# Decay sums with a stationary triangle, and a higher priority for the small inverses, in a two-layer hybrid decoder trunk

## The chip, the cores and the metric

The kernel runs as one program on one core of a Trainium2 chip. The metric is the device time of one execution in microseconds (us). Before the change it is 1251.22 us, the median of three runs that lie between 1250.65 and 1251.36 us. One further execution, made under the hardware profiler, took 1249.48 us; all rows of "the profile" come from that one.

## The reference

The reference computes two layers over 256 tokens of width 1024 in float32. Each layer is a half-step SwiGLU, a layer norm, three token mixers on one shared input projection (a gated delta rule, a sliding-window attention with sinks and an attention over a memory), gates and an output projection, a layer norm, a second half-step SwiGLU and a layer norm. The change concerns the gated delta rule with 4 heads. Cut to what matters:

```python
g = -jnp.exp(a_log) * jax.nn.softplus(a + dt_bias)        # log decay, one number per token and head
g = jnp.cumsum(g, axis=-1)                                # within a chunk
decay = jnp.exp(jnp.where(tril, g[..., :, None] - g[..., None, :], NEG_INF))
a = jnp.where(strict, jnp.einsum('bhncd,bhnsd->bhncs', k_beta, k) * decay, 0.0)
sol = lax.linalg.triangular_solve(a + jnp.eye(C), rhs, left_side=True, lower=True, unit_diagonal=True)
qk = jnp.where(tril, jnp.einsum('bhncd,bhnsd->bhncs', q, k) * decay, 0.0)
```

The kernel uses chunks of 128 tokens, so two chunks (c = 0 and 1) per layer. For each head and chunk it needs the 128x128 matrix of decay sums: the sum of g over the tokens that lie after token i and up to token j. That matrix is masked and put through an exponential. The triangular solve is replaced by the explicit inverse of the 128x128 unit triangle, made from its 16x16 blocks by doubling: 16 to 32, 32 to 64, 64 to 128.

## The kernel before

TensorE does nearly everything in products of type fp32r, each float32 matrix split into a high part and a rest: `split` (L124) makes the high part on ScalarE (a cast) and the rest on VectorE (a subtraction), both of type fp32r, and three products stand for one (`mm3`). The weights, 1024 columns of 128 partitions at a time, come through `unit` (L104): a DMA on SyncE's queue into one of four `raw` buffers, then the split into `whi` and `wlo`, which have five buffers each. Its instructions stand 300 places ahead of their place in the program.

The order of the instructions on each engine is worked out at build time by a planner. It simulates the program with its own costs, and whenever an engine is free it takes the ready instruction with the smallest place in the program, where a place can be moved ahead by an offset (`tc.high_priority(offset=...)`). `tc.issue_after` adds single edges of order. On the chip each engine then goes through its list in that order. Within the mixers all products of TensorE are pinned in program order (`pe`, L129, with `pinned[0]` set in `mixers`, L560), so the planner orders only the other engines there. `weave` (L145) runs a large projection as a generator and calls small steps between its parts; that is where the products of the delta rule stand in TensorE's order.

The decay sums. A chain of small operations on VectorE ends in `g` (L718, 128 tokens x 2 chunks x 4 heads). GpSimd then makes, for each chunk, a tile `gm` of 128x4x128 numbers: the strict triangle `mlt` times g of the token, one copy per head (L758). `spread(c)` (L737) runs four float32 products, one per head, with `gm` of that head as the stationary operand and the triangle of ones `tri` as the moving one; the sums land in one `sm` bank of PSUM. VectorE adds the mask (L743), ScalarE takes the exponential (L744). `gm` and the result are the two halves of one tile `TM[c]`, in the buffers `w2` and `w3`. `spread(0)` and `spread(1)` stand at steps 2 and 3 of the last small projection (L976). `products` (L746) then makes the matrices `AK`.

The inverses. `inverses` (L922) makes the 16x16 blocks on GpSimd. `doubling(c)` (L985) has four stages for each chunk; each runs some 32x32 products and then moves the results out of PSUM: a copy on ScalarE (L993), a subtraction and a transposition on VectorE (L999, L1000), copies on ScalarE (L1008), and in the last stage scaled copies on ScalarE (L1017, L1019, L1021) and copies on GpSimd (L1023). `double` (L1028) runs one stage for both chunks. `lower_products` (L1040) and `upper_products` (L1049) do the last step with 64x64 products and copies on ScalarE (L1046, L1047, L1056). They stand between the parts of the second gates' projection and the second branch's projection: stages of `double` at steps 1, 3, 5 and 7 of the gates (L1189), `lower_products` at step 8, `upper_products` inside the branch.

Around the same time run the window attention's probabilities: `w_scores` ends in exponentials and scalings on ScalarE (L860, L863), `w_leave` (L889) transposes on VectorE (L893) and sends the tile to DRAM by GpSimd's DMA queue (L896), `w_back` (L900) reads it back (`pt`, L906), and `w_values` (L908) uses it on TensorE.

Of the kernel before, what the change touches and what calls it, by code (L numbers as in the profile page):

```python
# [10 lines left out]
F32 = mybir.dt.float32  # L11
F32R = mybir.dt.float32r
I32 = mybir.dt.int32
AF = mybir.ActivationFunctionType
ALU = mybir.AluOpType
AX = mybir.AxisListType

P = 128
# [14 lines left out]
MAGIC = 0x5F3759DF  # L33
AHEAD = 300
HOLD = 4


@with_exitstack
def tile_trunk(ctx, tc, x, xT, mem, memT_, wst, lnp, memln, cvw, rows, cst, out):
    nc = tc.nc  # L40
# [3 lines left out]
    pc = ctx.enter_context(tc.tile_pool(name="pc", bufs=1))  # L44
    praw = ctx.enter_context(tc.tile_pool(name="praw", bufs=4))
    pu = ctx.enter_context(tc.tile_pool(name="pu", bufs=1))
# [8 lines left out]
    def nm(s):  # L55
        uid[0] += 1
        return f"{s}_{uid[0]}"
# [4 lines left out]
    def T(pool, shape, tag, dt=F32, bufs=None):  # L62
        pool = pn if pool is pu and tag in NEAR else pool
        kw = {} if bufs is None else {"bufs": bufs}
        return pool.tile(shape, dt, tag=tag, name=nm(tag), **kw)
# [7 lines left out]
    def sm():  # L73
        return T(psS, [P, 512], "sm")

    def load(dst, src):

        tc.keep_in_program_order(nc.sync.dma_start(dst, src))  # L78
# [3 lines left out]
    tri = cs[:, C_TRI:C_TRI + P]  # L82
    mlt = cs[:, C_LT:C_LT + P]
    dtm = cs[:, C_DTM:C_DTM + P]

    def over4(ap):
        return ap.unsqueeze(1).to_broadcast([P, 4, ap.shape[-1]])
# [41 lines left out]
    def pe(ins):  # L129

        return tc.keep_in_program_order(ins) if pinned[0] else ins

    def matmul(*a, **k):
        return pe(nc.tensor.matmul(*a, **k))  # L134
# [330 lines left out]
    def begin(nxt, hT):  # L465
        nxt.first(hT, 0)
        nxt.first(hT, 1)
        nxt.out(0, nxt.bank)
# [91 lines left out]
    def mixers(l, hT, mkT, mv_, post0, post):  # L560
# [122 lines left out]
        sh = [P, 2, 4]  # L683

        def col(tag):
            return T(pu, sh, tag)
# [11 lines left out]
        t = col("spt")  # L698
# [18 lines left out]
        g = col("g")  # L717
# [12 lines left out]
            nc.vector.tensor_scalar(neg1, eg[:, 0, 1, :], -1.0, None, ALU.mult)  # L730
            nc.vector.tensor_tensor(ktok, ktok, ks.unsqueeze(2).to_broadcast([P, 4, P]), op=ALU.mult)

        TM = [T(pu, [P, 2, 4, P], f"w{2 + c}") for c in range(2)]
        AK = [T(pu, [P, 4, 2, P], f"u{12 + c}") for c in range(2)]
        hb = lambda ap: ap.unsqueeze(2).to_broadcast([P, 4, P])

        def spread(c):  # L737

            gm, dt = TM[c][:, 0], TM[c][:, 1]
            ps = sm().rearrange("p (h c) -> p h c", h=4)  # L740
            for h in range(4):
                matmul(ps[:, h, :], gm[:, h, :], tri, start=True, stop=True)
            nc.vector.tensor_tensor(dt, ps, over4(dtm), op=ALU.add)  # L743
            nc.scalar.activation(dt, dt, AF.Exp)  # L744

        def products(c, hh):  # L746
# [6 lines left out]
            for j in range(2):  # L753
                h = 2 * hh + j
                nc.vector.scalar_tensor_tensor(AK[c][:, h], TM[c][:, 1][:, h, :].unsqueeze(1).to_broadcast([P, 2, P]), cS[:, c, h:h + 1], ps[:, j], op0=ALU.mult, op1=ALU.mult)

        for c in range(2):
            nc.gpsimd.tensor_tensor(TM[c][:, 0], over4(mlt), hb(g[:, c, :]), op=ALU.mult)  # L758


        xq = (T(pu, [P, 4, S], "u4", F32R), T(pu, [P, 4, S], "u6", F32R))
# [42 lines left out]
        def x_back():  # L804
            pT = prs[2] = T(p2, [P, 2, 4, 4, 32], "pt")
            for kb in range(2):
                with tc.issue_after(late["pool"]):
                    late["pool"] = nc.gpsimd.dma_start(pT[:, kb].rearrange("p a h x -> p (a h x)"), left_x[0][4 * kb:4 * kb + 4].rearrange("m x a c -> (m x) (a c)")).ins
# [113 lines left out]
        def inverses():  # L922
# [11 lines left out]
            x_back()  # L934
            tm = [t.rearrange("p a h c -> p (a h c)") for t in TM]
            parts = [tm[0][:, 0:512], tm[0][:, 512:1024], tm[1][:, 0:512]]
# [25 lines left out]
        X64, X32, Y32 = (W[:, a:b].rearrange("p (c h i) -> p c h i", c=2, h=4) for a, b in ((0, 512), (512, 768), (768, 1024)))  # L962
        Y = T(pu, [P, 2, 4, P], "w1")
# [21 lines left out]
        def doubling(c):  # L985
            B, M = AK[c][:, :, 0, :], TM[c][:, 1]
            Yc = Y[:, c]
            M32 = M[:, :, 0:32]
            ps = part()
            for h in range(4):  # L990
                for q in qd:
                    matmul(ps[q, h], L32[q, c, h], X32[q, c, h], start=True, stop=True)
            nc.scalar.copy(M32, ps)  # L993
            yield
            ps = part()
            for h in range(4):
                for q in qd:
                    matmul(ps[q, h], M32[q, h], Y32[q, c, h], start=True, stop=True)
            nc.vector.tensor_tensor(Y32[:, c], Y32[:, c], ps, op=ALU.subtract)  # L999
            late["dve"] = nc.vector.transpose(W[:, 512 + c * P:512 + c * P + P], W[:, 768 + c * P:768 + c * P + P]).ins  # L1000
            yield
            pairs = ((qd[0], qd[1]), (qd[2], qd[3]))
            ps = part()
            for h in range(4):
                for e, o in pairs:
                    matmul(ps[o, h], B[e, h, o], X32[e, c, h], start=True, stop=True)
            for e, o in pairs:
                pairs_ = nc.scalar.copy(M[o, :, e], ps[o]).ins  # L1008
            late["pairs"] = pairs_
            yield  # L1010
            ps = part()
            e, o = pairs[0]
            for h in range(4):
                for a, b in pairs:
                    matmul(ps[a, h], M[b, h, a], Y32[b, c, h], start=True, stop=True)
                matmul(ps[o, h], Y32[o, c, h], M[o, h, e], start=True, stop=True)
            nc.scalar.mul(X64[o, c, :, e], ps[o], -1.0)  # L1017
            for q in qd[:2]:
                nc.scalar.copy(X64[q, c, :, q], X32[q, c])  # L1019
            for a, b in (pairs if c == 0 else pairs[::-1]):  # L1020
                nc.scalar.mul(Yc[a, :, b], ps[a], -1.0)  # L1021
            for q in (qd if c == 0 else qd[::-1]):
                late["pool"] = nc.gpsimd.tensor_copy(Yc[q, :, q], Y32[q, c]).ins  # L1023
            yield

        stages = [doubling(c) for c in (1, 0)]

        def double():  # L1028
            for d in stages:
                next(d)  # L1030

        up, dn = slice(0, 64), slice(64, P)

# [5 lines left out]

        def lower_products():  # L1040

            pa, pb = (sm().rearrange("p (h c) -> p h c", h=4) for _ in range(2))
            for h in range(4):
                matmul(pa[dn, h, up], AK[0][up, h, 0, dn], X64[up, 0, h], start=True, stop=True)
                matmul(pb[up, h, dn], AK[1][dn, h, 0, up], Y[dn, 1, h, dn], start=True, stop=True)
            nc.scalar.copy(TM[0][dn, 1, :, up], pa[dn, :, up])  # L1046
            nc.scalar.copy(TM[1][up, 1, :, dn], pb[up, :, dn])  # L1047

        def upper_products():  # L1049

            pa, pb = (sm().rearrange("p (h c) -> p h c", h=4) for _ in range(2))
            for h in range(4):
                matmul(pa[up, h, dn], TM[0][dn, 1, h, up], Y[dn, 0, h, dn], start=True, stop=True)
                matmul(pb[up, h, dn], X64[up, 1, h], TM[1][up, 1, h, dn], start=True, stop=True)
            for c, ps in enumerate((pa, pb)):
                nc.scalar.mul(Y[up, c, :, dn], ps[up, :, dn], -1.0)  # L1056

        def begin_inverse():

# [191 lines left out]
    ps = sm()  # L1251
# [6 lines left out]
    def xres(tb):  # L1258
        load(hres[tb], x[tb * P:(tb + 1) * P, :])

    def small():
        load(rw, rows.rearrange("l r -> (l r)").partition_broadcast(P))
        load(cw, cvw)

    ends = None
    for l in range(NL):
        mT = []
        mid = memory_T(mT, l)
        if l == 0:

            mid[2] = lambda: load(cs, cst)
            more = {4: lambda *a: xres(0), 6: lambda *a: xres(1), 8: lambda *a: small()}
        post = Post(lnp[l, 0, 0], lnp[l, 0, 1], bounce=True)
        f1.rest(hT, 4, [((pu, "u0"), (pu, "u1")), ((pu, "u2"), (pu, "u3"))], post, mid, ends, {} if l else more)
        kv = memory_kv(mT, post)
        if l == 0:
            nc.scalar.activation(nea, rw[:, :, 8:12], AF.Exp)
            nc.vector.tensor_scalar(nea, nea, -1.0, None, ALU.mult)
        post2 = Post(lnp[l, 1, 0], lnp[l, 1, 1])
        mixers(l, post.hT, *kv, post, post2)  # L1280
        f2 = Ffn()
        begin(f2, post2.hT)
        last = l == NL - 1
        post = Post(lnp[l, 2, 0], lnp[l, 2, 1], last)
        f2.rest(post2.hT, 6, [((pu, a), (pu, b)) for a, b in (("u0", "u1"), ("u2", "u3"), ("u4", "u5"), ("u6", "u13"))], post, behind=post2.end)
        ends = post.end
        if not last:
            f1, hT = Ffn(), post.hT
            begin(f1, hT)
# [87 lines left out]
```

## Time and profile before

| What | Value |
|---|---|
| time, median of three runs | 1251.22 us (1250.65 to 1251.36) |
| time of the profiled execution | 1249.48 us |
| its span, first to last instruction | 1247.3 us |
| TensorE matmul busy | 1236.5 us, 99% |
| VectorE, ScalarE, GpSimd busy | 887.6, 655.4, 271.5 us |
| granted TensorE clock | 0.998 |

A row of the timeline gives the start in us from the span's start, the time taken, the engine, the line of the kernel, the operation and its operands, and how many instructions are merged; behind it in brackets the idle time of the engine before it and what ended it. PE is TensorE's matmul, PEld its weight load, DVE VectorE, ACT ScalarE, POOL GpSimd. The ends of matmuls are modelled and they overlap, so the distance between the starts of two neighbouring rows, divided by the count, is what one matmul costs the stream. A float32 product appears as two records, an fp32r product as one. A row of a group gives the count, the busy time, the mean ns of one, and the idle time before; a row of waits gives the time waited in total, the number of waits and the longest one.

### The profile page before, as it was taken

How to read it: one execution, taken by the hardware profiler on the slowest of the kernel's cores; microseconds unless marked ns; L12 is line 12 of the kernel's file. 1: busy time of each engine (PE TensorE's matmuls, PEld its weight loads, DVE VectorE, ACT ScalarE, POOL GpSimd, SP SyncE). 2: the span in 40 equal slices, each digit the busy share in tenths (PEclk: the TensorE clock that was granted, in tenths of full speed). 3: DMA queues.
4: the chain of work that ended last, by engine and by line, in shares of the span. 5: the costliest groups of instructions: out<-in, count | busy, mean ns of one | idle time of the engine just before them, and what ended most of it. 6: DMA issues, size and time to landing. Idle time of an engine off the chain costs nothing.

```text
span 1247.3 us, 18730 instructions
## 1 busy us (share of the span) xinstructions
PE 1236.5 (99%) x6812; PEld 1052.6 (84%) x6812; DVE 887.6 (71%) x1316; ACT 655.4 (53%) x976; POOL 271.5 (22%) x481
## 2 busy tenths in 40 slices
PE   9999999999999999999999999999999999999997
PEld 6888889999878888888888888899988788888886
DVE  6688567887768876665676665769869688666555
ACT  6456545656665544444455554456657644454541
POOL 1232102003751102221012220020046411122100
PEclk9999999999999999999999999999999999999999
DMA  8988866755675848886668886676566566688771
GB/s 296 320 267 279 259 228 202 239 171 179 184 242 169 269 140 257 240 242 220 220 207 241 262 255 216 215 238 207 170 192 214 177 215 213 204 243 240 242 230 74
DMA packets 83275, 276.73 MB, mean 222 GB/s; under 512 B 13776, under 2 KB 15216, under 8 KB 83184
## 3 DMA queue, kind: packets, MB, share of 16 engines
q1 hardware_dynamic: 66320, 232.40, 58.0%
q0 software_dynamic: 16720, 43.02, 12.0%
q8 instruction: 53, 0.87, 0.3%
q14 instruction: 38, 0.31, 0.1%
q10 hardware_dynamic: 144, 0.13, 0.0%
HBM read 253.77 MB, written 21.73 MB: 221 GB/s over the span
## 4 chain that ended last, share of the span: by engine, by line
PE 99%; DMA 0%; DVE 0%; SPq 0%; issue 0%; ACT 0%; DVEq 0%
PE acc L134 88%; PE at L134 4%; PE sm L134 3%; PE sm L137 1%; PE acc L332 1%; PE acc L333 1%; PE acc L335 1%; DMA raw<-in_wst_dram 0%; PE at L137 0%; DVE h L291 0%; DVE h L296 0%; SPq L115 0%; SPq L78 0%; ACT whi L125 0%; DVE bnst L277 0%
## 5 line engine op out<-in xcount | busy, mean ns | idle before, releaser
L125 DVE TENSOR_TENSOR wlo<-raw,whi 128x1024 fp32r<-128x1024 f32 (+2 forms) x405 | 486.4, 1209 | 252.1 <-ACT whi L125 249.7
L125 ACT CAST whi<-raw 128x1024 fp32r<-128x1024 f32 (+2 forms) x405 | 413.4, 1029 | 379.7 <-PE acc L134 293.6
L134 PE MATMUL acc<-whi,hT 128*128 128x512 f32 (+1 forms) x1824 | 559.9, 385 | 0.7 <-ACT whi L125 0.7
L134 PEld LDWEIGHTS acc<-whi,hT 128*128 128x128 f32 x1824 | 339.9, 188 | 70.1 <-ACT whi L125 2.7
L134 PE MATMUL acc<-wlo,hT 128*128 128x512 f32 (+1 forms) x912 | 350.1, 384 | 0.0
L134 PE MATMUL acc<-whi,u 128*128 128x512 f32 x812 | 259.0, 392 | 0.0
L134 PEld LDWEIGHTS acc<-wlo,hT 128*128 128x128 f32 x912 | 171.3, 188 | 32.9 <-DVE wlo L125 0.8
L134 PEld LDWEIGHTS acc<-whi,u 128*128 128x128 f32 x812 | 152.3, 188 | 33.8 <-issue 1.6
L362 POOL DMA_DIRECT2D tr<-t x176 | 96.0, 552 | 307.8 <-DVE t L356 307.6
L134 PE MATMUL acc<-wlo,u 128*128 128x512 f32 x406 | 158.2, 390 | 0.0
L134 PE MATMUL acc<-hT,whi 128*128 128x256 f32 x672 | 121.8, 284 | 0.0
L134 PEld LDWEIGHTS acc<-hT,whi 128*128 128x128 f32 x672 | 104.7, 192 | 0.0
L134 PE MATMUL acc<-hT,wlo 128*128 128x256 f32 x336 | 95.1, 283 | 0.0
L134 PEld LDWEIGHTS acc<-wlo,u 128*128 128x128 f32 x406 | 76.3, 188 | 15.5
L363 POOL DMA_DIRECT2D pt<-tr x44 | 24.6, 558 | 197.1 <-DMA tr<-t 143.0
L134 PEld LDWEIGHTS acc<-hT,wlo 128*128 128x128 f32 x336 | 64.4, 192 | 0.0
L353 ACT ACTIVATE t<-acc 128x256 f32<-128x256 f32 x88 | 33.4, 379 | 37.3 <-PE acc L134 37.2
L134 PE MATMUL acc<-u,u 128*128 128x512 f32 x186 | 46.4, 394 | 0.0
L354 DVE TENSOR_TENSOR t<-t,acc 128x256 f32<-128x256 f32 x88 | 36.7, 417 | 8.1 <-ACT t L353 3.8
L134 PEld LDWEIGHTS acc<-u,u 128*128 128x128 f32 x186 | 34.6, 188 | 7.5
L125 DVE TENSOR_TENSOR u<-pt,u 128x512 fp32r<-128x512 f32 x46 | 30.3, 659 | 13.2 <-ACT u L125 13.2
L125 ACT CAST u<-pt 128x512 fp32r<-128x512 f32 x46 | 28.1, 611 | 21.3 <-DMA pt<-tr 12.3
(264 smaller groups left out, 1190.4 us busy)
## 6 DMA issues: line engine op xcount, KB each, us to landing
raw<-in_wst_dram SPq DMA_DIRECT2D x409, 512.0 KB, 4.5
tr<-t POOLq DMA_DIRECT2D x176, 64.0 KB, 3.9
pt<-tr POOLq DMA_DIRECT2D x44, 256.0 KB, 5.2
raw<-in_wst_dram SPq DMA_DIRECT2D x16, 324.0 KB, 4.4
gB<-in_lnp_dram SPq DMA_DIRECT2D x6, 512.0 KB, 6.0
bB<-in_lnp_dram SPq DMA_DIRECT2D x6, 512.0 KB, 6.2
pt<-tw POOLq DMA_DIRECT2D x12, 256.0 KB, 5.6
tn<-pp POOLq DMA_DIRECT2D x16, 128.0 KB, 4.1
```

Source lines behind the costliest of these rows:

```text
L125: return nc.scalar.copy(hi, src).ins, nc.vector.tensor_tensor(lo, src, hi.bitcast(F32), op=ALU.subtract).ins
L134: return pe(nc.tensor.matmul(*a, **k))
L137: return pe(nc.tensor.transpose(*a))
L332: nc.tensor.matmul(ps, hT[0][:, k, ts], hi[:, c], start=k == 0, stop=False)
L333: nc.tensor.matmul(ps, hT[0][:, k, ts], lo[:, c], start=False, stop=False)
L335: nc.tensor.matmul(ps, hT[1][:, k, ts], hi[:, c], start=False, stop=k == KD - 1)
L353: act = nc.scalar.activation(t[:, :, tb, :], g, AF.Silu).ins
L354: ins = nc.vector.tensor_tensor(t[:, :, tb, :], t[:, :, tb, :], u, op=ALU.mult).ins
L362: nc.gpsimd.dma_start(d[:, :, q].rearrange("b c x -> c b x"), z[32 * q:32 * q + 32].rearrange("c (b x) -> c b x", b=4))
L363: back = nc.gpsimd.dma_start(y, d.rearrange("b c q x -> (b c) (q x)")).ins
```

## The change

The stationary operand of the decay sums becomes the strict triangle, rounded to fp32r once for the whole program (`mltr`, one copy on ScalarE in layer 0), and the moving operand becomes the triangle of ones times g of the token, for all four heads in one row of 512 columns. The log decay g is split into a high part `gh` and a rest `gl` (two small operations on VectorE), GpSimd makes two moving tiles for each chunk, and two products accumulate. `TM[c]` becomes a tile of its own that takes the same buffer once the moving tiles have been used. Besides, everything in `double`, `lower_products` and `upper_products` is put 120 places ahead in the planner's order.

```diff
+SOON = 120
...
+    mltr = pc.tile([P, P], F32R, name="mltr")
...
-        TM = [T(pu, [P, 2, 4, P], f"w{2 + c}") for c in range(2)]
+        TM, gm = [None, None], [T(pu, [P, 2, 4, P], f"w{2 + c}", F32R) for c in range(2)]
...
         def spread(c):
 
-            gm, dt = TM[c][:, 0], TM[c][:, 1]
             ps = sm().rearrange("p (h c) -> p h c", h=4)
-            for h in range(4):
-                matmul(ps[:, h, :], gm[:, h, :], tri, start=True, stop=True)
+            for i in range(2):
+                matmul(ps, mltr, gm[c][:, i], start=i == 0, stop=i == 1)
+            TM[c] = T(pu, [P, 2, 4, P], f"w{2 + c}")
+            dt = TM[c][:, 1]
             nc.vector.tensor_tensor(dt, ps, over4(dtm), op=ALU.add)
...
+        gh, gl = (T(pu, sh, tag, F32R) for tag in ("gh", "gl"))
+        nc.vector.tensor_copy(gh, g)
+        nc.vector.tensor_tensor(gl, g, gh.bitcast(F32), op=ALU.subtract)
         for c in range(2):
-            nc.gpsimd.tensor_tensor(TM[c][:, 0], over4(mlt), hb(g[:, c, :]), op=ALU.mult)
+            for i, t in enumerate((gh, gl)):
+                nc.gpsimd.tensor_tensor(gm[c][:, i], over4(tri), hb(t.bitcast(F32)[:, c, :]), op=ALU.mult)
...
         def double():
-            for d in stages:
-                next(d)
+            with tc.high_priority(offset=SOON):
+                for d in stages:
+                    next(d)
...
         def lower_products():
+            with tc.high_priority(offset=SOON):
                 pa, pb = (sm().rearrange("p (h c) -> p h c", h=4) for _ in range(2))
...
         def upper_products():
+            with tc.high_priority(offset=SOON):
                 pa, pb = (sm().rearrange("p (h c) -> p h c", h=4) for _ in range(2))
...
         if l == 0:
+            nc.scalar.copy(mltr, mlt)
             nc.scalar.activation(nea, rw[:, :, 8:12], AF.Exp)
```

More of the change, by code (lines that the diff above doesn't have):

```diff
@@ L1040, in lower_products @@
         def lower_products():
[L1042 to L1047, printed above, removed]
-        def upper_products():
[L1051 to L1056, printed above, removed]
+            with tc.high_priority(offset=SOON):
+                pa, pb = (sm().rearrange("p (h c) -> p h c", h=4) for _ in range(2))
+                for h in range(4):
+                    matmul(pa[dn, h, up], AK[0][up, h, 0, dn], X64[up, 0, h], start=True, stop=True)
+                    matmul(pb[up, h, dn], AK[1][dn, h, 0, up], Y[dn, 1, h, dn], start=True, stop=True)
+                nc.scalar.copy(TM[0][dn, 1, :, up], pa[dn, :, up])
+                nc.scalar.copy(TM[1][up, 1, :, dn], pb[up, :, dn])
+        def upper_products():
+            with tc.high_priority(offset=SOON):
+                pa, pb = (sm().rearrange("p (h c) -> p h c", h=4) for _ in range(2))
+                for h in range(4):
+                    matmul(pa[up, h, dn], TM[0][dn, 1, h, up], Y[dn, 0, h, dn], start=True, stop=True)
+                    matmul(pb[up, h, dn], X64[up, 1, h], TM[1][up, 1, h, dn], start=True, stop=True)
+                for c, ps in enumerate((pa, pb)):
+                    nc.scalar.mul(Y[up, c, :, dn], ps[up, :, dn], -1.0)
         def begin_inverse():
```

## The prediction, made before the changed kernel was run

> **What bounds the kernel now.** I read the page first, then who waits for whom, then the timeline around the decay sums. From the page:
>
> ```profile
> span 1247.3 us, 18730 instructions
> ...
> PE 1236.5 (99%) x6812; PEld 1052.6 (84%) x6812; DVE 887.6 (71%) x1316; ACT 655.4 (53%) x976; POOL 271.5 (22%) x481
> ...
> PE 99%; DMA 0%; DVE 0%; SPq 0%; issue 0%; ACT 0%; DVEq 0%
> ```
>
> The chain that ended last is TensorE for 99% of the span. A busy share of 99% alone could hide small gaps, since the modelled ends of matmuls overlap, so the waits of TensorE matter more; the view of waits, kept to that engine, has three rows in all (total us, times, longest):
>
> ```profile
> PE sm L1253 <- DVE pp L1250: 1.5, 1, 1.5
> PE acc L134 <- ACT whi L125: 0.7, 2, 0.4
> PE sm L137 <- issue: 0.3, 1, 0.3
> ```
>
> None of them is a product of the decay sums or of the inverses. L1253 is the warm-up at the start, `acc` the first weights, L137 a transposition. So the kernel is one unbroken stream of products, and whatever the change takes out of that stream comes off the time nearly whole, while work on the other engines counts only if it makes the stream wait.
>
> **What the sums cost in the stream.** All 16 float32 products of `spread` (4 heads, 2 chunks, 2 layers) in one group, then the first layer's two blocks in TensorE's timeline (`sm<-cs,w` is the block):
>
> ```profile
> L134 PE MATMUL sm<-cs,w 128*128 128x128 f32 x32 | 4.2, 274 | 0.0
> ```
>
> ```profile
> 279.71 1.05 PE L134 MATMUL sm<-cs,w 128*128 128x128 f32 x8
> 280.52 1.66 PE L134 MATMUL at<-u,u 128*128 128x256 f32 x12
> ```
>
> ```profile
> 284.78 0.28 PE L134 MATMUL acc<-hT,wlo 128*128 128x256 f32 x1
> 284.90 1.05 PE L134 MATMUL sm<-cs,w 128*128 128x128 f32 x8
> 285.71 0.48 PE L134 MATMUL acc<-hT,whi 128*128 128x256 f32 x2
> 286.03 0.29 PE L134 MATMUL acc<-hT,wlo 128*128 128x256 f32 x1
> ```
>
> Each block is 8 records, two for each product, and 32 records are four blocks. The 274 ns of one record is latency; what the stream pays is the distance of starts. From 284.90 to 285.71 that is 0.81 us. The two products behind it then take 0.32 us (285.71 to 286.03) where one product of this kind takes 0.12 us (284.78 to 284.90), so 0.08 us more is paid there: **0.89 us a block**, 3.56 us for the four. The block of 279.71 has the same 0.81 us.
>
> The new block is two products of fp32r with 512 columns. What these cost in the stream is shown right behind:
>
> ```profile
> 290.92 0.63 PE L134 MATMUL acc<-whi,hT 128*128 128x512 f32 x2
> 291.39 0.39 PE L134 MATMUL acc<-wlo,hT 128*128 128x512 f32 x1
> ```
>
> Two products from 290.92 to 291.39, 0.23 us each; **0.46 us a block**. There each product loads its own stationary tile and the load is hidden, as the new loads of `mltr` will be. Saved: 0.89 - 0.46 = 0.43 us a block, 4 x 0.43 = **1.7 us**. The Trainium skill, page "TensorE: Matmul & The Clock Gate", section "Back-to-back issue gap", gives N/2.4 + 2.5 ns, an estimate of 0.216 us for 512 columns; by it the sum would be 4 x (0.89 - 0.43) = 1.8 us. The rows have 0.23, and I take the rows.
>
> **What it adds, and whether that is covered.** On VectorE two operations of 128x8, `gh` and `gl`; on GpSimd, per layer, four multiplications where there were two; on ScalarE one copy of 128x128 in the whole program. The rows around the first layer's sums, VectorE, then GpSimd with its group, then the second layer's GpSimd and TensorE:
>
> ```profile
> 276.01 0.16 DVE L718 TENSOR_TENSOR g<-spp,nea 128x8 f32<-128x8 f32 x1
> 276.09 0.41 DVE L125 TENSOR_TENSOR swk<-acc,swk 64x256 fp32r<-64x256 f32 x1
> 276.93 0.43 DVE L125 TENSOR_TENSOR swk<-acc,swk 64x256 fp32r<-64x256 f32 x1 [0.43 <-ACT swk L125]
> 278.00 1.37 DVE L125 TENSOR_TENSOR wlo<-raw,whi 128x1024 fp32r<-128x1024 f32 x1 [0.65 <-ACT whi L125]
> ```
>
> ```profile
> 276.25 2.04 POOL L758 TENSOR_TENSOR w<-cs,g 128x512 f32<-128x512 f32 x2 [48.53 <-DVE g L718]
> ```
>
> ```profile
> L758 POOL TENSOR_TENSOR w<-cs,g 128x512 f32<-128x512 f32 x4 | 4.1, 1040 | 96.8 <-DVE g L718 96.8
> ```
>
> ```profile
> 893.57 2.04 POOL L758 TENSOR_TENSOR w<-cs,g 128x512 f32<-128x512 f32 x2 [48.27 <-DVE g L718]
> ```
>
> ```profile
> 897.03 1.05 PE L134 MATMUL sm<-cs,w 128*128 128x128 f32 x8
> ```
>
> `gh` and `gl` take as long as `g` itself, 0.16 us each by L718; no row has a GpSimd operation that writes fp32r, so I take the 1.04 us of L758, whose operands have the same size. TensorE needs the first tile at 279.71 and the second at 279.71 + 0.23 = 279.94. Today it is made by 276.25 + 1.04 = 277.29, 2.4 us early. After the change it depends on where the planner puts `gh` and `gl` on VectorE. There is room beside the two `swk` operations, with 0.43 us of idle time before the second and 0.65 us behind it, and in the program the two stand ahead of `swk`. With `gh` behind the first `swk` (276.09 + 0.41 = 276.50, done by 276.7) GpSimd makes the high tile until 277.7 and the low tile until 278.8, some **1.1 us early**. With both straight behind `g` it is 1.5 us. So I cost this at nothing, but the cover is thin; the first rival is what it costs if it is gone. In the second layer the same distance, 897.03 - 893.57 = 3.46 us, lies between GpSimd's start and the block, as here 279.71 - 276.25, so both layers go the same way. Chunk 1's tiles end by about 281, or 283 if GpSimd is held up twice, and TensorE wants them at 284.90 less 0.43. GpSimd's next own work is far: it sat idle for up to 14.3 us before the masks of the inverses.
>
> ```profile
> POOL l L789 <- DVE u L755: 28.7, 2, 14.3
> ```
>
> The one copy of `mltr` stands ahead of the first mixers on an engine that is busy 53%. Its price is bounded by nothing and by the 0.27 us of one small ScalarE copy (two in the row of L1021 below take 0.55).
>
> **The moved part.** TensorE's order is pinned there, so its products stay where they are. What moves are the copies on ScalarE, the updates on VectorE and the last stage's copies on GpSimd. How early are they today? ScalarE's last copy of the doubling and what it waits for at the end, and TensorE's products that use them:
>
> ```profile
> 359.86 0.55 ACT L1021 ACTIVATE w<-sm 32x128 f32<-32x128 f32 x2
> ```
>
> ```profile
> 367.85 0.65 ACT L1056 ACTIVATE w<-sm 64x256 f32<-64x256 f32 x2 [3.54 <-PE sm L134]
> ```
>
> ```profile
> 361.54 0.68 PE L134 MATMUL sm<-w,u 64*64 64x64 f32 x16
> ```
>
> ```profile
> 370.42 1.05 PE L134 MATMUL sm<-u,w 128*128 128x128 f32 x8
> ```
>
> The last copies before `lower_products` end at 360.41, 1.1 us before 361.54. Those of `upper_products` end at 368.50, 1.9 us before 370.42. Nothing waits for them, so putting them sooner **gains nothing**. What can it lose? A copy that stands too early in ScalarE's list waits there for TensorE, and the weights' casts behind it wait too. L1056 does that today for 3.54 us, and TensorE does not stall. The casts in turn mostly wait for TensorE to free one of the five buffers:
>
> ```profile
> ACT whi L125 <- PE acc L134: 293.6, 246, 2.3
> ```
>
> They run as early as the buffers let them, so a copy of 0.3 us ahead of a cast is absorbed. Zero is the value; the bounds are nothing and the second rival.
>
> **Sum.** 0 + 0 - 1.7 us. The profiled execution took 1249.48 us, 2.2 us around its span of 1247.3; I expect 1247.8 with a span of 1245.6. The median of the runs stood 1.7 us above the profiled one, so the median forecast is 1251.2 - 1.7 = **1249.5 us**, 0.14% less. A measurement of this kernel tells about 0.2%, or 2.5 us, from no change, so this counts as the same.
>
> **Rival 1, ends slower: the low tile is late.** If the planner lets the weights' `wlo` of 278.00 go before `gh` and `gl`, they run from 279.37 on, the first ends at 279.5, and two multiplications of 1.04 us end at 281.6: TensorE stands 1.65 us in each layer, +3.3 - 1.7 = +1.6, **1252.8 us**. It turns into a loss where the stall passes 0.87 us a layer. For it: `wlo` stands 300 places ahead and takes VectorE as soon as its cast is done. Against it: the 0.43 and 0.65 us gaps show that it was not ready in time. A milder form needs no late `gl`. GpSimd can be held up by VectorE itself:
>
> ```profile
> L1023 POOL COPY w<-w x16: 283/288/1336, 349.2 to 971.4; 32x128 f32<-32x128 f32 x16
> ```
>
> ```profile
> 352.44 1.34 POOL L1023 COPY w<-w 32x128 f32<-32x128 f32 x1
> ```
>
> ```profile
> 352.40 1.23 DVE L125 TENSOR_TENSOR wlo<-raw,whi 128x1024 fp32r<-128x1024 f32 x1 [0.99 <-ACT whi L125]
> ```
>
> A copy of 0.29 us that begins just behind a `wlo` takes 1.34 us, until that one is done. If the low tile begins after 278.00, it stands until 279.37 and ends at 280.4: 0.5 us late a layer, 1250.5 us. In my placing it begins at 277.7, only 0.3 us before. The Trainium skill, page "SBUF — State Buffer", section "Who interferes with whom", states this as a rule: a VectorE operation with two inputs in SBUF and a GpSimd one that reads SBUF exclude each other, the second to issue waits. By that rule, the trace agrees (1.34 against 0.29 us). I give the late form 0.05 and the mild one 0.12.
>
> **Rival 2: the probabilities' way through DRAM slips.** ScalarE's scaling L863 feeds a transposition, GpSimd's DMAs (L896), their way back (L906) and the products of `w_values(1)`:
>
> ```profile
> 352.27 1.70 ACT L863 ACTIVATE pp<-pp,sums 128x256 f32<-128x256 f32 x4
> 354.00 1.09 ACT L1008 COPY w<-sm 32x128 f32<-32x128 f32 x4
> ```
>
> ```profile
> 355.61 2.30 POOL L896 DMA_DIRECT2D tw<-bB  x4 [1.83 <-DVE bB L893]
> ```
>
> ```profile
> L906 POOL DMA_DIRECT2D pt<-tw x1: 536/536/536, 363.8 to 363.8; - x1
> DMA to landing us min/median/max: 4.1/4.1/4.1
> ```
>
> ```profile
> 367.75 1.94 PE L134 MATMUL at<-pt,swv 128*64 128x512 f32 x8
> ```
>
> The last read lands at 363.8 + 4.1 = 367.9; TensorE uses it in the second half of a block that begins at 367.75 and lasts 1.9 us, so at about 368.7. The slack is 0.8 us. If the copies of L1008 (1.09 us) overtake L863, TensorE waits 0.3 us a layer; with the four of L1019 and L1021 that could come too, 1.4 us: 1249.5 + 0.6 to 2.8, say **1250.6 us**. Against it: by my count of the code L1008 stands some 126 places behind L863, and the offset is 120, so it stays just behind. Chance 0.10.
>
> **Rival 3: it doesn't do what it says.** Were the two products run at the float32 pace, 0.89 us for 512 columns, a block would take 1.78 us: +0.89 x 4 = +3.6, **1254.8 us**. The tiles are of type fp32r, and all such products in the rows run at 0.23; chance 0.02.
>
> **How the numbers follow.** My forecast 0.66 (within 1248.9 to 1250.2); rival 1 0.17, rival 2 0.10, rival 3 0.02; 0.05 is left for more gain than I see, through another order that the planner finds. The range 1248.7 to 1251.8 holds the forecast, the mild form of rival 1 and most of rival 2, and leaves out the late form, rival 3 and the unseen gain. Faster by over 0.2% needs 1248.7 or less: the unseen gain and the lower edge of my case, 0.10. Slower by over 0.2% needs 1253.7 or more: rival 3 and the far ends of rivals 1 and 2, 0.06. The rest, 0.84, is the same.
>
> **What would show it.** Right: two `sm` records of 128x512 per block, 0.46 us from the first to what follows, no new row among TensorE's waits, GpSimd's four multiplications of about 1.04 us, the last low tile of chunk 0 done ahead of its product. Wrong: a wait of `sm` on GpSimd (rival 1), of `at` on a DMA at `w_values(1)` (rival 2), a distance over 0.23 us between the two products (rival 3), or a wait of TensorE for `whi` in the gates.

## The result, and the profile after

| | before | after |
|---|---|---|
| median, four runs each on one chip | 1250.93 us | 1259.82 us (1258.84 to 1260.18) |
| ratio to before, 95% interval | | 1.0075 [1.0063, 1.0088] |
| profiled execution, its span | 1249.48, 1247.3 us | 1260.18, 1258.3 us |

The change makes the kernel slower, by 0.75%, where 0.14% of gain was forecast. The page of the changed kernel, its rows of the busy times and of the chain that ended last:

```profile
PE 1238.6 (98%) x6788; PEld 1051.3 (84%) x6788; DVE 890.6 (71%) x1320; ACT 654.7 (52%) x977; POOL 275.5 (22%) x485
...
PE 83%; DMA 6%; DVE 4%; POOL 3%; issue 2%; ACT 2%; SPq 0%; DVEq 0%; POOLq 0%; ACTq 0%
```

The unbroken chain of TensorE (99% before) is broken: 15% of it now leads over DMAs, VectorE, GpSimd and ScalarE, and 2% is issue. TensorE has two more busy microseconds in the records although it has 24 records fewer; the reason comes below. Where it stands still is in the view of TensorE's waits (total us, times, longest), after:

```profile
PE at L137 <- DMA pt<-tw: 8.5, 2, 4.5
PE sm L1264 <- DVE pp L1261: 1.5, 1, 1.5
...
PE sm L140 <- POOL u L1187: 0.6, 1, 0.6
```

The second row is the warm-up, as before. The first is new and is most of the loss: `at` is the block of `w_values(1)`, `pt` the probabilities read back from DRAM, once in each layer. (Lines have shifted by 3 to 11: L134 is L137 now, the scalings L863 are L871, the copies of the pairs L1008 are L1016, the transposition L893 is L901, the DMAs L896 and L906 are L904 and L914. L1187 is a multiplication on GpSimd. In the experiments the lines shift again by a few.) The decay sums themselves did what was forecast. TensorE's timeline after, the sums of chunk 0 and what follows them:

```profile
279.52 0.63 PE L137 MATMUL sm<-w,mltr 128*128 128x512 f32 x2
279.99 1.22 PE L137 MATMUL at<-u,u 128*128 128x256 f32 x9
```

The block takes 0.47 us from start to start, where it took 0.81 and delayed its successors. GpSimd's timeline after, the first three of its four multiplications:

```profile
276.46 1.04 POOL L766 TENSOR_TENSOR w<-cs,gh 128x512 fp32r<-128x512 f32 x1 [48.99 <-DVE gh L762]
277.46 1.04 POOL L766 TENSOR_TENSOR w<-cs,gl 128x512 fp32r<-128x512 f32 x1
278.46 2.02 POOL L766 TENSOR_TENSOR w<-cs,gh 128x512 fp32r<-128x512 f32 x1
```

Chunk 0's low tile is done at 277.46 + 1.04 = 278.50. Its product, the second of the block, starts at about 279.52 + 0.23 = 279.75, so the tile is 1.2 us early. No product of the sums waits.

**The stall.** TensorE's timeline at the end of layer 1's inverses, after, and then before (the block of `at` stands in the prediction at 367.75):

```profile
366.12 0.68 PE L137 MATMUL sm<-w,w 64*64 64x64 f32 x16
370.86 3.26 PE L137 MATMUL at<-pt,swv 128*64 128x512 f32 x8 [4.05 <-DMA pt<-tw]
```

```profile
367.14 0.68 PE L134 MATMUL sm<-w,w 64*64 64x64 f32 x16
```

TensorE comes to this place 1.02 us sooner than before (366.12 against 367.14; 0.19 of it was there before the sums, 279.52 against 279.71) and then stands for 4.05 us. In layer 2 it is 4.48 us:

```profile
994.36 3.29 PE L137 MATMUL at<-pt,swv 128*64 128x512 f32 x8 [4.48 <-DMA pt<-tw]
997.58 0.78 PE L137 MATMUL acc<-whi,u 128*128 128x512 f32 x1
```

After each stall the same eight products take 3.26 and 3.29 us where they took 1.94 before, though their data is there. The view of windows after says why (span of time; busy us of PE, PEld, DVE, ACT and POOL with counts; then the granted clock, DMA share and GB/s):

```profile
370.20:373.50 3.30, 2.64 (x8) 0.85 (x8) 0.00 (x0) 0.00 (x0) 1.65 (x3) 0.50 0.04 8
373.70:376.00 2.30, 2.30 (x15) 1.76 (x14) 1.35 (x3) 0.79 (x3) 0.52 (x2) 1.00 0.07 5
```

The granted clock is 0.50 from some 0.7 us before the end of the stall, for some 3.4 us, and then 1.00 again. Those slower products are why TensorE is busy for longer. The bill: 8.5 us of waiting for `pt`, 1.32 + 1.35 us of slower blocks, 0.6 us of a transposition that waits for GpSimd (L1187), less 1.7 us of the sums, makes 10.1 of the 11.0 us by which the span grew. Products behind the second block that still ran at half clock (0.78 us at 997.58) are part of the rest.

**Why the data is late.** ScalarE's timeline after, from the blocks of X64 (L1027) to the last scaling (L871):

```profile
347.54 0.61 ACT L1027 COPY w<-w 32x128 f32<-32x128 f32 x2 [1.28 <-DVE w L1008]
...
349.84 0.50 ACT L868 ACTIVATE pp<-pp,mx 128x256 f32<-128x256 f32 x1
...
351.82 1.03 ACT L128 CAST whi<-raw 128x1024 fp32r<-128x1024 f32 x1
352.88 1.10 ACT L1016 COPY w<-sm 32x128 f32<-32x128 f32 x4
354.00 1.31 ACT L871 ACTIVATE pp<-pp,sums 128x256 f32<-128x256 f32 x3
355.22 1.03 ACT L128 CAST whi<-raw 128x1024 fp32r<-128x1024 f32 x1
356.15 0.51 ACT L871 ACTIVATE pp<-pp,sums 128x256 f32<-128x256 f32 x1
```

Before, the scalings stood at 352.27 and the pairs at 354.00. Now the pairs are first, the scalings begin at 354.00, and a cast of the weights has come between the third and the fourth, so they end at 356.66 and not at 353.97. VectorE after, and GpSimd after:

```profile
356.28 1.23 DVE L128 TENSOR_TENSOR wlo<-raw,whi 128x1024 fp32r<-128x1024 f32 x1 [2.17 <-ACT whi L128]
357.43 1.30 DVE L901 STREAM_TRANSPOSE bB<-pp 128x512 f32<-128x512 f32 x2
```

```profile
359.02 2.31 POOL L904 DMA_DIRECT2D tw<-bB  x4 [7.04 <-DVE bB L901]
...
366.44 1.07 POOL L914 DMA_DIRECT2D pt<-tw  x2 [4.01 <-DMA tw<-bB]
```

The low part of that same cast takes VectorE from 356.28, the transposition goes behind it (357.43), and the DMAs to DRAM start at 359.02, 3.41 us later than the 355.61 of before. This is the place and the mechanism of the second rival, at three times the upper end of its price (8.5 us of waiting against 2.8), and without what the clock adds.

### The profile page after: what moved, and what is told of

Read it like the earlier page. It is cut to its first block, busy times and chain, and to the rows that moved or that the text cites. A ratio compares the mean times of both kernels' runs of the same rounds, so it can differ in the third digit from the quotient of the medians.

```text
span 1258.3 us, 18689 instructions
## 1 busy us (share of the span) xinstructions
PE 1238.6 (98%) x6788; PEld 1051.3 (84%) x6788; DVE 890.6 (71%) x1320; ACT 654.7 (52%) x977; POOL 275.5 (22%) x485
## 4 chain that ended last, share of the span: by engine, by line
PE 83%; DMA 6%; DVE 4%; POOL 3%; issue 2%; ACT 2%; SPq 0%; DVEq 0%; POOLq 0%; ACTq 0%
PE acc L137 76%; PE at L137 3%; DMA raw<-in_wst_dram 2%; DVE wlo L128 2%; PE sm L137 1%; POOL t L962 1%; DMA w<-dr 1%; PE sm L140 1%; PE acc L335 1%; ACT whi L128 1%; POOL t L961 1%; DMA tw<-bB 1%; PE acc L336 1%; PE acc L338 1%; DMA pt<-tw 1%
## 5 line engine op out<-in xcount | busy, mean ns | idle before, releaser
L137 PE MATMUL acc<-whi,hT 128*128 128x512 f32 (+1 forms) x1824 | 559.6, 385 | 0.6 <-ACT whi L128 0.6
L137 PEld LDWEIGHTS acc<-whi,hT 128*128 128x128 f32 x1824 | 339.8, 188 | 69.6 <-ACT whi L128 2.3
L137 PE MATMUL acc<-wlo,hT 128*128 128x512 f32 (+1 forms) x912 | 350.3, 384 | 0.0
L137 PE MATMUL acc<-whi,u 128*128 128x512 f32 x812 | 259.2, 392 | 0.0
L137 PEld LDWEIGHTS acc<-wlo,hT 128*128 128x128 f32 x912 | 171.3, 188 | 33.5 <-DVE wlo L128 1.3
L137 PEld LDWEIGHTS acc<-whi,u 128*128 128x128 f32 x812 | 152.4, 188 | 35.1 <-issue 2.8
L137 PE MATMUL acc<-wlo,u 128*128 128x512 f32 x406 | 158.3, 390 | 0.0
L137 PE MATMUL acc<-hT,whi 128*128 128x256 f32 x672 | 121.6, 283 | 0.0
L137 PEld LDWEIGHTS acc<-hT,whi 128*128 128x128 f32 x672 | 104.9, 192 | 0.2
L137 PE MATMUL acc<-hT,wlo 128*128 128x256 f32 x336 | 95.1, 283 | 0.0
L137 PEld LDWEIGHTS acc<-wlo,u 128*128 128x128 f32 x406 | 76.4, 188 | 15.9 <-DVE wlo L128 0.5
L137 PEld LDWEIGHTS acc<-hT,wlo 128*128 128x128 f32 x336 | 64.5, 192 | 0.0
L137 PE MATMUL acc<-u,u 128*128 128x512 f32 x186 | 46.4, 394 | 0.0
L137 PEld LDWEIGHTS acc<-u,u 128*128 128x128 f32 x186 | 34.6, 188 | 7.5
```

## The experiments

Medians stand beside a kernel before on the same chip: 1249.90 us for the first four experiments, 1250.56 for the next four, 1249.89 for the last four. Ratios have 95% intervals; they are worked out over all the runs and can differ from the quotient of the two medians (0.9982 against 0.9989 in experiment 6). `SOON` is the offset of 120 places.

**1. The sums alone.** All three priority blocks are taken out.

```diff
-            with tc.high_priority(offset=SOON):
+            with nullcontext():
```

> The new decay sums with no priority for the inverses. My theory: the 11 us that the changed kernel's span gained come from the moved priority alone, through ScalarE's and VectorE's order ahead of the window probabilities' way through DRAM. Then this kernel has the stream of before less 0.43 us for each of four blocks: 1249.2 us against 1250.9, ratio 0.9986 (0.998 to 0.9995), and no wait of TensorE for a DMA at w_values. Rival: the new sums do it themselves (GpSimd's longer multiplications hold up VectorE, whose chain is then late): then this kernel is slow by itself, 1257 to 1262 us, with the two waits for the DMA.

Measured: 1250.13 us, ratio 1.0003 [0.9994, 1.0012]. The loss is gone, so the sums do not cause it, but the 1.7 us of gain do not show either. The rows of its TensorE waits for the work around the inverses:

```profile
PE at L137 <- DMA pt<-tw: 0.8, 1, 0.8
PE sm L140 <- POOL u L1187: 0.6, 1, 0.6
PE sm L137 <- ACT w L1025: 0.3, 1, 0.3
PE sm L137 <- ACT w L1029: 0.3, 1, 0.3
```

L1025 and L1029 are the scaled copies of the inverses' last stage. None of these four rows was there before. Together they are 2.0 us, about what the sums save, in a profile whose 1251.77 us lie above the median. Experiments 6 to 9 test whether this is where the gain went.

**2. The priority alone.** The kernel before with the three blocks of `high_priority` and nothing else.

```diff
         def double():
-            for d in stages:
-                next(d)
+            with tc.high_priority(offset=SOON):
+                for d in stages:
+                    next(d)
```

(and the same around the bodies of `lower_products` and `upper_products`)

> The priority alone, on the decay sums of before. My theory: the two waits of 4.2 and 4.7 us for the DMA at w_values(1) and the slow clock behind them are all there, and the 1.7 us of the sums are missing: 1261.5 us (1260 to 1263), ratio 1.0085. Rival, the sums do it: 1251 us, ratio 1.000. Rival, only both together do it: 1251 us too, and the sums alone near 1249.

Measured: 1259.10 us, ratio 1.0075 [1.0059, 1.0090], the ratio of the whole change, and below the 1260 to 1263 us expected. Its first row of TensorE's waits is

```profile
PE at L135 <- DMA pt<-tw: 6.3, 2, 3.2
```

**The priority is the loss**, with or without the sums. The waits are 2.2 us shorter than in the changed kernel. TensorE, without what the sums save (2 x 0.43 us a layer), comes to them later, which is 1.7 us of it.

**3. and 4. Only ScalarE's copies, only VectorE's updates.** The sums, with the priority around single operations of `doubling` and nowhere else: in the one around every copy of ScalarE, in the other around the subtraction and the transposition of VectorE.

```diff
-            nc.scalar.copy(M32, ps)
+            with tc.high_priority(offset=SOON):
+                nc.scalar.copy(M32, ps)
```

```diff
-            nc.vector.tensor_tensor(Y32[:, c], Y32[:, c], ps, op=ALU.subtract)
+            with tc.high_priority(offset=SOON):
+                nc.vector.tensor_tensor(Y32[:, c], Y32[:, c], ps, op=ALU.subtract)
```

> The new sums, and of the priority only that of ScalarE's copies in the four doubling stages. In the planned order three copies of the last stage, one cast of weights and two of the third stage's copies then stand ahead of the last three scalings of the probabilities (0.9 + 1.05 + 0.55 = 2.5 us). My theory, that ScalarE's share is the larger one: 2.5 us less the 0.8 us of slack is a wait of 1.7 us in each layer, 1249.2 + 3.4 = 1252.6 us (1251 to 1255). If VectorE's order does it all, this stays at 1249.2.

> The new sums, and of the priority only that of VectorE's updates and transpositions in the doubling stages; in the planned order GpSimd's copies of the last stage come ahead of four DMA issues as a consequence, and three copies of ScalarE's ahead of the exponentials. My theory: the maximum of the probabilities is 0.8 us later and the exponentials 0.9 us more, less 0.8 us of slack: a wait of 0.9 us in each layer, 1249.2 + 1.8 = 1251.0 us (1249.5 to 1254). If VectorE's order does it all, 1259 to 1260.

Measured: 1254.21 us, ratio 1.0037 [1.0024, 1.0051] for ScalarE's; 1255.53 us, ratio 1.0050 [1.0034, 1.0067] for VectorE's, above the 1249.5 to 1254 us expected. Each half alone costs something, but not the same thing. The first rows of TensorE's waits, ScalarE's first, then VectorE's:

```profile
PE at L137 <- DMA pt<-tw: 4.5, 3, 2.5
```

```profile
PE sm L137 <- ACT w L1018: 2.9, 2, 1.6
PE at L137 <- DMA pt<-tw: 2.6, 2, 2.1
```

VectorE's profile is of the longest of its four runs (1259.27 us). With VectorE's updates alone ahead, the planner set ScalarE's copies of the pairs (L1018 here) further back, to 357.37 in layer 1 where they stood at 354.00 before, and TensorE waits for these 2.9 us. That is a loss that the whole change doesn't have, so the two halves cannot simply be added, although their ratios add up to something near the whole. Experiment 4 is therefore no measure of VectorE's share; 10 and 11 come closer.

**5., 6. and 7. Without the wait for the probabilities.** `w_values(1)` reads tile 0's probabilities, which were there long before, in the changed kernel, in the sums alone and in the kernel before. This leaves out the second tile's probabilities from the output, so these kernels only serve to time the wait.

```diff
-                    o, w = pso[hs]..., wpT[tb][kb].rearrange(...)
+                    o, w = pso[hs]..., wpT[0][0].rearrange(...)
```

> Both parts of the change, but the products of w_values(1) read the probabilities of tile 0 (there for 20 us) in place of those of tile 1; everything that makes and carries tile 1's probabilities still runs, only TensorE no longer waits for it. The output of the window attention is therefore another. If the wait for the way through DRAM is the whole loss, the two stalls of some 4.2 and 4.7 us and the slow clock behind them go, and what is left is the sums' gain less a wait of 0.7 us: 1249.3 to 1250.0 us, ratio about 0.999. If the new order also delays TensorE elsewhere (casts of the weights late), a good part stays: 1253 or more.

> The sums alone, with the same cut of the wait. In the sums alone the profile showed 0.8 us of wait for that DMA and some 1.7 us for the inverses' copies. If the wait for DRAM ate the gain, this comes to the full gain: ratio 0.9986 (1248.2 beside a kernel before of 1249.9). If the inverses' copies ate the larger part: 0.9993 to 0.9997. If the sums save nothing in the stream after all: 1.0003 as without the cut.

> The kernel before, with the same cut of the wait, as a control. Its profile shows no wait of TensorE there, so every theory expects the time of before: ratio 1.0000, within 0.0008. If it is faster by over 0.1%, then the kernel before pays for this wait in most of its runs, and the profiled one was a lucky one.

Measured: 1251.45 us, ratio 1.0005 [0.9995, 1.0016] for the changed kernel; 1249.15, 0.9982 [0.9968, 0.9995] for the sums alone; 1250.30, 0.9995 [0.9985, 1.0006] for the kernel before. Two things follow.

The changed kernel loses its loss with this one wait: 1.0075 becomes 1.0005, although the DMAs to DRAM start as late (at 359.39 in its profile). **The way of the probabilities is the path by which the priority costs time.** Its 1251.45 us are above the 1249.3 to 1250.0 expected. What stays against the sums alone is in the rows of its waits, of which L1128 is a step of the delta rule on VectorE:

```profile
PE sm L137 <- DVE w L1128: 1.4, 2, 0.8
PE sm L140 <- POOL u L1187: 0.6, 1, 0.6
```

And the sums do save what was forecast, once nothing else holds TensorE: experiment 6 over experiment 7 is 0.9982 / 0.9995, or 1.6 us. The whole of TensorE's waits in the sums with the cut:

```profile
PE sm L1264 <- DVE pp L1261: 1.5, 1, 1.5
PE acc L137 <- ACT whi L128: 0.5, 1, 0.5
```

The profiled spans, 1246.1 us here and 1247.9 us in the kernel before with the same cut, differ by 1.8 us.

**8. and 9. The scores sooner.** The scores `w_scores(1, 1)` move from step 1 of the second gates to the last step of the first branch, with the sums alone and in the kernel before.

```diff
-            3: [lambda: w_leave0(1), leave_v, begin_inverse, lambda: w_scores(1, 0)]})
+            3: [lambda: w_leave0(1), leave_v, begin_inverse, lambda: w_scores(1, 0)],
+            4: [lambda: w_scores(1, 1)]})
         weave(gates(1), {
-            1: [double, lambda: w_scores(1, 1)],
+            1: [double],
```

> The sums alone, with the scores w_scores(1, 1) moved 2.7 us of products sooner (to the last step of the first branch, where they stood behind step 1 of the second gates). If the sums' gain is eaten because the chain behind the scores has no slack for a stream that comes 0.87 us sooner, the gain appears: ratio 0.9985 to 0.9992. If the chain is set by ScalarE's order (the weights' casts ahead of it, which wait for their own DMA) and not by when the scores are there, nothing changes: 1.0003.

> The kernel before with the scores w_scores(1, 1) moved to the last step of the first branch, as a control for the sums with the same move. In the kernel before TensorE does not wait for what follows from these scores, so if the sums' gain is what the move sets free, this is 1.0000 within 0.0008. If the move is worth something by itself, whatever the sums, this is 0.9985 as with the sums, and the sums would be worth nothing.

Measured: 1248.38 us, ratio 0.9983 [0.9972, 0.9993] with the sums; 1249.87 us, 0.9998 [0.9989, 1.0006] without. The move is worth nothing by itself and gives the sums their gain: 1.0003 without it, 0.9983 with it, and the two intervals lie apart. In the profile of experiment 8 TensorE's wait for `pt` is gone (0.8 us in experiment 1). **This kernel computes the same and beats both**: the sums, the order of before, and the scores a little sooner.

What ate the gain in experiment 1 shows in ScalarE's timeline ahead of layer 2's exponentials, experiment 1, then before:

```profile
957.71 1.05 ACT L128 CAST whi<-raw 128x1024 fp32r<-128x1024 f32 x1 [3.07 <-DMA raw<-in_wst_dram]
```

```profile
955.80 1.05 ACT L125 CAST whi<-raw 128x1024 fp32r<-128x1024 f32 x1 [0.82 <-DMA raw<-in_wst_dram]
```

ScalarE takes its list in order. A weights' cast that waits 3.07 us for its DMA holds the exponentials behind it, whose input VectorE had finished at 956.92, until 958.76, and with them the way through DRAM. If that part of the chain goes by the weights' arrival and not by TensorE, a TensorE that comes sooner only runs into it. One profile shows this, so that it holds in most runs of experiment 1 is argued, not shown; and why the DMA came later is open.

**10. and 11. The copies behind the scalings.** Both parts of the change, but ScalarE's copies of the pairs are held until the last scaling has been issued; in experiment 10 the blocks of X64 as well.

```diff
             for e, o in pairs:
-                pairs_ = nc.scalar.copy(M[o, :, e], ps[o]).ins
+                with tc.issue_after(late["act"]):
+                    pairs_ = nc.scalar.copy(M[o, :, e], ps[o]).ins
...
             for q in qd[:2]:
-                nc.scalar.copy(X64[q, c, :, q], X32[q, c])
+                with tc.issue_after(late["act"]):
+                    nc.scalar.copy(X64[q, c, :, q], X32[q, c])
```

> Both parts of the change, but ScalarE's copies of the pairs and of the blocks of X64 are held behind the last scaling of the probabilities; VectorE's updates stay ahead as in the change. If the chain of the probabilities is late because ScalarE's copies overtook the exponentials (with 1.3 us of wait for VectorE in front) and the scalings, its DMAs start again at about 356 us where the change had 359.0, and the ratio is 0.999 to 1.001. If VectorE's updates ahead of the maximum's sign change (0.8 us later in the changed kernel) are a cause of their own, some 0.8 us a layer of stall stay and the clock slows behind it: 1.002 to 1.003.

> As the last, but only the copies of the pairs are held; the blocks of X64 stay ahead of the exponentials. The pairs take 1.1 us ahead of the scalings and let a weights' cast of 1.0 us in between them; without these the DMAs start 1.1 to 2.1 us sooner than the 359.0 us of the change, and the stalls of 4.2 and 4.7 us shrink by as much: ratio 1.004 to 1.0055. If the pairs are the whole cause, 1.000; if the blocks of X64 are, 1.007.

Measured: 1251.51 us, ratio 1.0009 [0.9998, 1.0020] with both held; 1250.94 us, 1.0004 [0.9996, 1.0013] with the pairs alone. I had expected 1.004 to 1.0055 of the pairs alone; **holding the four copies of the pairs brings the ratio back to that of the sums alone** (1.0003). ScalarE and GpSimd in experiment 11:

```profile
351.58 1.03 ACT L128 CAST whi<-raw 128x1024 fp32r<-128x1024 f32 x1
352.52 1.70 ACT L871 ACTIVATE pp<-pp,sums 128x256 f32<-128x256 f32 x4
354.25 1.09 ACT L1017 COPY w<-sm 32x128 f32<-32x128 f32 x4
```

```profile
355.85 2.30 POOL L904 DMA_DIRECT2D tw<-bB  x4 [4.14 <-DVE bB L901]
```

The exponentials are as late as in the changed kernel (the cast behind them begins at 351.58 against 351.82), with X64 ahead of them, and yet the DMAs start at 355.85 and not at 359.02. So 1.1 us of copies cost nearly 3 us of the difference of 3.17: the scalings begin 1.48 us sooner (352.52 against 354.00; 0.24 of it was there at the cast), take 0.96 less (1.70 against 2.66) as no cast comes between them, and the remaining 0.7 is the transposition, which no longer finds VectorE taken by that cast's low part. The order of X64 and of VectorE's updates was nearly free.

Experiment 10 settles less: its runs spread from 1248.5 to 1256.9 us, and the profiled one is the longest (span 1254.9). In it the wait for `pt` is gone too. TensorE waits for VectorE's transposition in the second stage (L1008) and for a scaled copy of the last one (L1026):

```profile
PE sm L137 <- DVE w L1008: 2.7, 2, 2.2
PE sm L137 <- ACT w L1026: 1.7, 2, 1.1
```

**12. Both parts, and the scores sooner.** The edit of experiment 8, on the changed kernel.

> Both parts of the change with the scores moved sooner. In the planned order ScalarE's scalings still stand behind the copies of the pairs, and those wait for TensorE's products of step 3, whose time the move does not change; the exponentials are no longer behind a copy that waits. So the stall shrinks by the 1.6 us of the exponentials at most, and the loss stays for the most part: ratio 1.003 to 1.0065. If the lateness comes of the scores being late and not of the order on ScalarE, the loss is gone: 0.999 to 1.000.

Measured: 1261.48 us, ratio 1.0091 [1.0076, 1.0106]; the 1.003 to 1.0065 expected was too low. It separates late scores from the order on ScalarE. ScalarE in it, and GpSimd:

```profile
349.94 1.21 ACT L1027 COPY w<-w 32x128 f32<-32x128 f32 x4
...
352.86 1.09 ACT L1016 COPY w<-sm 32x128 f32<-32x128 f32 x4
353.98 1.31 ACT L871 ACTIVATE pp<-pp,sums 128x256 f32<-128x256 f32 x3
```

```profile
358.99 1.15 POOL L904 DMA_DIRECT2D tw<-bB  x2 [7.85 <-DVE bB L901]
```

The exponentials are over when L1027 begins at 349.94, 1.9 us sooner than in the changed kernel (351.82), and the scalings still begin at 353.98, the DMAs at 358.99 (359.02 in the changed kernel). VectorE had the sums ready at 351.33. Between the exponentials and the scalings stand X64, a gate (L1165), a cast and the pairs, four microseconds of other work. So what stands ahead of the scalings in ScalarE's list sets their time; when the scores are there does not.

Its ratio is above the 1.0075 of the whole change, with intervals that overlap, and the profile is of the longest of the six runs (1265.58 us). In it the last reads from DRAM start 1.35 us later than in the changed kernel (367.79 against 366.44), though the DMAs to DRAM start together; the reason is open.

## Why the prediction was wrong

**What bounds the kernel: right.** TensorE's stream, with no slack of its own. But "whatever the change takes out of that stream comes off the time nearly whole" holds only while the next thing that TensorE needs isn't just as tight. In the sums alone it was, and 1.7 us became nothing (1.0003), until the wait was cut (0.9982) or the scores moved (0.9983).

**The sums: right.** 0.47 us a block measured, 0.46 forecast; 1.8 us between the spans of experiments 6 and 7 against the 1.7 of the sum.

**What it adds: right.** The low tile of chunk 0 was ready 1.2 us early (1.1 forecast); GpSimd's third multiplication took 2.02 us, held up by a low part of the weights on VectorE, in chunk 1 where it cost nothing. The first rival and the third did not come.

**The moved part: wrong, and this is the step that failed.** "Zero is the value" was put on it. The runs showed +0.75% for it alone (experiment 2): the copies of the pairs, put ahead of the scalings, delay the DMAs of the probabilities by nearly 3 us (experiment 11), and in the changed kernel TensorE then stands for 4.05 and 4.48 us and runs slow behind it. The zero rested on two arguments. One was that nothing waits for the copies, so moving them is free. It looked at who waits for what is moved, and too little at what the moved work is put in front of. The other was that the casts absorb "a copy of 0.3 us ahead of a cast". A cast can; a chain of scaling, transposition, two DMAs and a product that is due cannot.

**The second rival: right in place and mechanism, wrong in its chance and size.** Three things in it failed.

- *The order.* "By my count of the code L1008 stands some 126 places behind L863, and the offset is 120, so it stays just behind." It did not stay: the pairs stand at 352.88 and the scalings at 354.00. Whether the count was off, or the planner, which also goes by when an operand is ready and an engine free, found the pairs ready first, no run shows. A count within 5% of the offset should have been an even chance, not 0.10.
- *The slack.* Its 0.8 us were right, but only for a TensorE that comes when it came before. The first half of the block shows it too. It needs the third of the four reads. GpSimd in the kernel before, then this one read's time from issue to landing (the read of 363.25), and that of the same read after (366.44):

```profile
363.25 1.06 POOL L906 DMA_DIRECT2D pt<-tw  x2 [3.74 <-DMA tw<-bB]
```

```profile
DMA to landing us min/median/max: 3.7/3.7/3.7
```

```profile
DMA to landing us min/median/max: 4.3/4.3/4.3
```

  Before, it lands at 363.25 + 3.7 = 366.95, 0.8 us ahead of the block of 367.75. By the forecast's own sum TensorE comes 2 x 0.43 = 0.86 us sooner, measured 1.02, so this slack was gone before anything slipped. The two halves of the change were costed each with the other at rest.
- *The price of the overtaking.* 1.1 us of copies were priced at 1.1 us. They delayed the DMAs by nearly 3 (3.17 between experiment 11 and the changed kernel, less the 0.24), since the shifted chain met a cast on ScalarE and its low part on VectorE that it had passed before. And a stall of 4 us cost another 1.3 us a layer in clock.

Put together for layer 1: the last pair of reads starts 366.44 - 363.25 = 3.19 us later, its first read takes 0.6 us longer, TensorE is there 1.02 us sooner, less 0.8 us of slack: 4.0 us by the rows, 4.05 measured. The rival's price with these terms would have been near 4 us a layer before the clock, not 0.3 to 1.4.

**What would show it: right.** The wait of `at` on a DMA at `w_values(1)` was named, and it is the first row of the waits.

## What to carry to other kernels

Raising the priority of work that nothing waits for is not free: on an engine that takes its list in order it pushes something back, so follow the work that is passed, through all its engines and queues, to its consumer, and take the slack there with the rest of the change in place. A gain on the critical engine spends the slack of everything that feeds it; check the feeds that go by their own clock (a DMA of weights, a way through DRAM) before counting the gain, and if one is short, start it sooner, as experiment 8 did. An operation that slips may slip past more than it was pushed by, since it lands behind work that it used to precede.

## What the runs showed of the hardware

**A stall costs more than its length.** After the 4.05 us without products the granted clock was 0.50 for some 3.4 us, in part still in the stall. How long a stall it takes differed. In the view of windows, experiment 2 behind its two stalls (3.2 us in layer 1, 3.1 in layer 2, by its row of waits above), then experiment 10 behind its longest one, of 2.2 us, and experiment 12 at the end of its longest, of 4.9 us:

```profile
371.30:374.30 3.00, 3.00 (x15) 1.51 (x16) 0.62 (x2) 0.60 (x2) 2.07 (x4) 1.00 0.05 3
991.50:994.50 3.00, 2.90 (x8) 0.86 (x8) 0.00 (x0) 0.00 (x0) 1.90 (x4) 0.50 0.04 4
```

```profile
973.60:976.90 3.30, 3.30 (x9) 2.53 (x9) 2.65 (x7) 3.30 (x10) 2.32 (x7) 0.50 0.70 215
```

```profile
369.40:376.00 6.60, 4.31 (x10) 1.45 (x11) 0.18 (x1) 0.37 (x1) 3.45 (x5) 0.50 0.25 75
```

Of the first three, the longest left the clock at 1.00 and the two shorter ones halved it. In experiment 12 it stayed halved for 6.6 us, about twice as long. The Trainium skill, page "TensorE: Matmul & The Clock Gate", section "What's actually happening", says that the clock falls to half after at least one idle window of about 3.4 us, and that the window runs free of the kernel. The 3.4 us of the slow stretch agree, and a window that runs free would fit that like stalls came out differently. That a whole idle window is needed does not agree with the 2.2 us in experiment 10, which are 2.9 us even with the 32x32 products behind them counted as idle (970.45 to 973.37).

**Engines hold each other up both ways.** The multiplication of 1.04 us on GpSimd took 2.02 beside a low part on VectorE, and that low part took longer as well. VectorE after:

```profile
277.81 1.77 DVE L128 TENSOR_TENSOR wlo<-raw,whi 128x1024 fp32r<-128x1024 f32 x1 [0.64 <-ACT whi L128]
```

1.77 us against the 1.22 to 1.23 of most of its kind. By the rule of the Trainium skill, page "SBUF — State Buffer", section "Who interferes with whom", that the prediction drew on, the second to issue waits; the trace agrees, and shows that VectorE is at times the second.
